# SSD stage with TensorE's small steps further apart, and the second diagonal product in the carried product's PSUM bank

## The chip, the cores and the metric

The kernel runs on one core of one Trainium2 chip, as one launch. The metric is the device time of that core in microseconds (us), as the median of several runs.

## The reference

Two layers of a decoder trunk on 512 tokens of width 1024, in float32. Layer 0 mixes tokens with a Mamba-2 SSD block, layer 1 with an HGRN2 block; each is followed by a layer norm, a squared-ReLU MLP, a second layer norm and a gated embedding. The change touches the SSD block alone:

```
def ssd_mixer(u, ...):                       # u: 512 x 1024; 4 chunks of 128 tokens
    z, xbc, dt = split(u @ w_in)             # z 2048, xbc 2048 + 512 + 512, dt 32 heads
    xs, bm, cm = split(silu(conv4(xbc)))     # causal depthwise convolution of width 4
    dt = softplus(dt + dt_bias); da = dt * -exp(a_log); xdt = xs * dt
    a_cs = cumsum(da) in each chunk
    cb = cm . bm                             # per group (4 groups of 8 heads), 128 x 128
    y_diag = (cb * exp(segsum(da))) @ xdt
    states = bm . (exp(a_cs[-1] - a_cs) * xdt)
    prev = scan over chunks: h * exp(a_cs[-1]) + states
    y_off = cm . prev * exp(a_cs)
    y = (y_diag + y_off + d_skip * xs) * silu(z)
    return rms_norm(y per group of 512) @ w_out
```

## The kernel before

A float32 weight or activation is split into a rounded high part and the rest (`split`, L113 on ScalarE and L115 on VectorE), and each product is made of three matmuls (`mm3`, L119 to L121). Weights come as units of 128x1024 by one load on SyncE's queue, three buffers deep (`raw`), and are copied to six buffers of high and low parts, far ahead of their use.

The SSD block works on channels as rows: 16 tiles of 128 channels (two heads) by 512 tokens. Each tile j has x (`xs`) and the gate (`sz`), made by `xz(j)`: eight steps of `mm3` for x, then convolution (L633 on ScalarE, three L636 on VectorE) and silu (L637), then eight steps for the gate and silu (L697). Each group of four tiles has B and C (`bc_group`, 16 steps) and `bc_prep`: B is transposed (L673) and copied (L675, ScalarE), B·C is multiplied (L679) into bank `py0` and masked (L681, VectorE). `partial(g, h)` is 16 steps of the output product of a finished group, each chunk added to `acc` by L812 on VectorE.

The SSD core of a tile has four small steps on TensorE:

- `enter(j)`: loads the cumulated decays (L709, 512 KB on SyncE's queue), transposes x into bank `pt` (L712); VectorE scales it to `xw` (L718) and `xdt` (L719, two buffers).
- `states(j)`: six matmuls into bank `pm` (L727); VectorE scans them over the chunks (L734, L736, L737); then the decay mask is made (eight L743 on VectorE, L746 on ScalarE, L747 on VectorE) and L752.
- `carried(j)`: multiplies C with the scanned states into bank `py1` (L759); VectorE takes it with L766.
- `diagonal(js)`: for one or two tiles the masked product (L778, 16 matmuls each), the first into `py0`, the second into `pm`; with `rms` the normalizing matmuls of a group follow (L828, bank `pt`, then L832 on ScalarE). VectorE and ScalarE finish y (L791 to L796, L817, L820).

TensorE's order is written by hand in `period(p, work, at)`: the large work is a list of generators that yield after each `mm3` (three matmuls, one unit), and `at` says after which unit which small step is issued. Periods 1 to 8 each take two tiles. In the kernel before, `head(j, n, step)` puts enter, states and carried at units n, n + 4 and n + 8 (with steps of 3 for tile 14). All other engines' instructions are put in order by a scheduler, which works from this order; on each engine they run strictly in that order.

Of the kernel before, what the change touches and what calls it, by code (L numbers as in the profile page):

```python
# [44 lines left out]
def trunk(ctx: ExitStack, tc, a):  # L45
# [13 lines left out]
    psy = pool("psy", 1, space=PSUM)  # L59
    psm = pool("psm", 1, space=PSUM)  # L60
# [7 lines left out]
    def mk(p, shape, tag, dt=F32, **kw):  # L68
        return p.tile(list(shape), dt, tag=tag, name=nm(tag), **kw)
# [19 lines left out]
    def tmp(tag, shape, dt=F32):  # L89
        return mk(phase[0], shape, tag, dt, bufs=phase[2].get(tag, 1))  # L90

    def bank(p, tag):
        return mk(p, [P, T], tag)

    def bc(ap, axis, n):
        v = ap.unsqueeze(axis)
        shape = list(v.shape)
        shape[axis] = n
        return v.to_broadcast(shape)
# [76 lines left out]
    cols, at = {}, 0  # L176
# [479 lines left out]
    def bc_group(g):  # L656
        new = []
        for which in range(2):
            ps = yield from projected(10 * g + which)
            t = tmp(("bm", "cm")[which], [P, T])  # L660
            conv_silu(ps, 16 + 4 * which + g, t)
            new.append(t)
            if g:
                yield
        bcm[:] = new
# [22 lines left out]
    def xz(j):  # L688
        d = tiles[j] = dict()
        ps = yield from projected(10 * (j // 4) + 2 + 2 * (j % 4))  # L690
        d["xs"] = tmp("xs", [P, T])
        conv_silu(ps, j, d["xs"])
        if j:
            yield
        ps = yield from projected(10 * (j // 4) + 3 + 2 * (j % 4))
        d["sz"] = tmp("sz", [P, T])
        nc.scalar.activation(d["sz"], ps, AF.Silu)  # L697
        if j:
            yield
        if j == 4:  # L700
            nc.sync.dma_start(acc, a["x"])
            for c in range(NCH):
                nc.vector.tensor_scalar(acc[:, c, :], acc[:, c, :], ALPHA, None, ALU.mult)

    def enter(j):

        d = tiles[j]
        d["csb"] = mk(w4, [P, 2, T], "a")
        nc.sync.dma_start(d["csb"], bass.AP(tensor=csd.tensor, offset=csd.offset + 2 * j * T, ap=[[0, P], [T, 2], [1, T]]))  # L709
        pt = bank(pst, "pt")  # L710
        for c in range(NCH):
            nc.tensor.transpose(pt[:, c * P : (c + 1) * P], d["xs"][:, c * P : (c + 1) * P], ident)  # L712
        dt_tok, w_tok, _ = toks
        d["xdt"] = tmp("xdt", [P, 8, 64])
        hs = slice(2 * j, 2 * j + 2)
        ptv = pt.rearrange("p (c h q) -> p c h q", c=NCH, h=2)
        d["xw"] = tmp("xw", [P, 3, 2, 64])
        nc.vector.tensor_mul(d["xw"], ptv[:, 0:3], bc(w_tok[:, 0:3, hs], 3, 64))  # L718
        nc.vector.tensor_mul(d["xdt"].rearrange("p (c h) q -> p c h q", c=NCH), ptv, bc(dt_tok[:, :, hs], 3, 64))  # L719

    def states(j):
        d = tiles[j]
        csb, cs_tok = d["csb"], toks[2]
        btok, cbm, cm = prep
        pst_ = bank(psm, "pm")
        for c in range(3):
            nc.tensor.matmul(  # L727
                pst_[:, c * P : (c + 1) * P], btok[:, c, :], d["xw"][:, c].rearrange("p h q -> p (h q)"), start=True, stop=True
            )
        cd = mk(sm, [P, 2, NCH], "cd")  # L730
        nc.scalar.activation(cd, csb.rearrange("p h (c l) -> p h c l", c=NCH)[:, :, :, P - 1], AF.Exp)
        pv = d["pv"] = tmp("pv", [P, 3, 2, 64])
        stv = pst_[:, : 3 * P].rearrange("p (c h q) -> p c h q", c=3, h=2)
        nc.vector.tensor_copy(pv[:, 0], stv[:, 0])  # L734
        for c in range(1, 3):
            nc.vector.tensor_mul(pv[:, c], pv[:, c - 1], bc(cd[:, :, c], 2, 64))  # L736
            nc.vector.tensor_add(pv[:, c], stv[:, c], pv[:, c])  # L737

        m = d["m"] = mk(w4, [P, 2, T], "b")
        for r in range(2):  # L740
            for c in range(NCH):
                sl = slice(c * P, (c + 1) * P)
                nc.vector.tensor_scalar(  # L743
                    m[:, r, sl], csb[:, r, sl], cs_tok[:, c, 2 * j + r : 2 * j + r + 1], 0.0, ALU.subtract, ALU.min
                )
        nc.scalar.activation(m, m, AF.Exp)  # L746
        nc.vector.tensor_mul(m, m, bc(cbm, 1, 2))  # L747

        d["ecs"] = tmp("ecs", [P, 3 * P])
        for r in range(2):  # L750
            rs = slice(64 * r, 64 * r + 64)
            nc.scalar.activation(d["ecs"][rs], csb[rs, r, P:], AF.Exp)  # L752

    def carried(j):
        d = tiles[j]
        cm = prep[2]
        yo = bank(psy, "py1")
        for c in range(1, NCH):
            nc.tensor.matmul(  # L759
                yo[:, c * P : (c + 1) * P],  # L760
                d["pv"][:, c - 1].rearrange("p h q -> p (h q)"),
                cm[:, c * P : (c + 1) * P],
                start=True,
                stop=True,
            )
        nc.vector.tensor_mul(d["ecs"], yo[:, P:], d["ecs"])  # L766
# [3 lines left out]
    def diagonal(js, rms=None):  # L770

        yds = []
        for n, j in enumerate(js):
            yd = bank(psm, "pm") if n else bank(psy, "py0")
            for c in range(NCH):
                sl = slice(c * P, (c + 1) * P)
                for r in range(2):
                    nc.tensor.matmul(  # L778
                        yd[64 * r : 64 * r + 64, sl], tiles[j]["xdt"][:, 2 * c + r, :], tiles[j]["m"][:, r, sl], start=True, stop=True
                    )  # L780
            yds.append(yd)
        if rms is not None:
            groups[rms]["ri"] = rms_group(groups[rms]["ss"])
        for j, yd in zip(js, yds):
            d = tiles.pop(j)
            if j % 4 == 0:
                groups[j // 4] = dict(ys=Split(4), ss=None)
            g = groups[j // 4]
            ys = g["ys"]
            y = tmp("y", [P, T])  # L790
            nc.vector.scalar_tensor_tensor(y, d["xs"], dskip[:, j : j + 1], yd, ALU.mult, ALU.add)  # L791
            nc.vector.tensor_add(y[:, P:], y[:, P:], d["ecs"])
            nc.vector.tensor_mul(y, y, d["sz"])
            w = snw[:, j : j + 1]
            nc.scalar.activation(ys.h(j % 4), y, AF.Copy, scale=w)
            nc.vector.scalar_tensor_tensor(ys.l(j % 4), y, w, f32(ys.h(j % 4)), ALU.mult, ALU.subtract)  # L796
            g["ss"] = sq_sum(y, g["ss"])
# [38 lines left out]
    def period(p, work, at):  # L836

        n = 0
        for item in work:
            for _ in item:  # L840
                n += 1
                for f in at.pop(n, ()):
                    f()
        assert not at, (p, n, at.keys())

    def head(j, n, step=4):
        return {n: [lambda: enter(j)], n + step: [lambda: states(j)], n + 2 * step: [lambda: carried(j)]}

    both = lambda js, rms=None: [lambda: diagonal(js, rms)]
    with tc.manual_schedule(engines={mybir.EngineType.PE}):  # L850
        period(0, [bc_group(0), xz(0), xz(1)], {})
        toks.extend(dt_tail())
        period(1, [xz(2), xz(3)], {8: [bc_prep], **head(0, 12), **head(1, 22)})
        period(2, [bc_group(1), xz(4), xz(5)], {1: both((0, 1)), **head(2, 3), **head(3, 14), 26: [bc_prep], 27: both((2, 3)), **head(4, 37)})
        for p in range(3, 8):
            i, b = 2 * p - 1, p // 2
            if p == 7:
                work = [partial(1, 1), xz(14), xz(15)]
                at = {**head(i, 1), 18: both((i - 1, i), 2), **head(14, 32, 3), 43: both((14,))}
            elif p % 2:  # L860
                work = [xz(i + 1), xz(i + 2)]
                work.insert(1, partial(b - 1, 0))
                at = {**head(i, 1), 15: both((i - 1, i), b - 1), **head(i + 1, 20)}
            else:
                work = [bc_group(b), xz(i + 1), xz(i + 2)]
                if p == 4:
                    work.insert(1, partial(0, 1))
                n = 16 * len(work) - 48
                at = {**head(i, 1), 14: both((i - 1, i)), 26: [bc_prep], **head(i + 1, 35 + n)}
            period(p, work, at)  # L870
        period(8, [partial(2, 0), partial(2, 1)], {**head(15, 1), 14: both((15,))})
    h_s, *after = norm(0)
    out_project(a["wso"][12:16], groups[3]["ys"], False, *after, scale=rms_group(groups[3]["ss"]))
    begin("mlp0")
# [427 lines left out]
```

## Time and profile before

| | us |
|---|---|
| median of 3 runs | 1446.43 (1445.96 to 1446.88) |
| time of the profiled execution | 1448.71 |
| its span, first to last instruction | 1446.8 |
| TensorE busy | 1421.9 |
| VectorE busy | 1055.4 |
| ScalarE busy | 781.8 |
| mean granted TensorE clock | 0.995 of full speed |

A page has the busy time by engine, the span in slices, the DMA queues, the chain that ended last, and groups of instructions with mean time and the idle time before them. In these, PE is TensorE, DVE is VectorE, ACT is ScalarE and SP is SyncE; L712 is line 712 of the kernel. Other answers of the trace are: who waited for whom in a stretch (us in total, times, longest us), busy time by stretch (for TensorE, its weight loads, VectorE, ScalarE and GpSimd, then the granted clock, the share and rate of DMA), groups by line (busy us, mean ns, then idle us before them), and the timeline (start in us, length in us, engine, line, operation, tiles written and read, count).

### The profile page before, as it was taken

The numbers are of one execution on the slowest core, as the hardware profiler recorded it, in microseconds if no ns is written. First come the engines' busy times: TensorE is split into PE (matmuls) and PEld (weight loads), VectorE is DVE, ScalarE is ACT, GpSimd is POOL, SyncE is SP. The second block draws the span as 40 slices with busy tenths as digits, with TensorE's granted clock in tenths as the row PEclk, the third lists the DMA queues.
The fourth block names the chain that finished last, engine by engine and source line by source line (L and its number), as shares of the span: only waits on it lengthen the run. The fifth ranks groups of instructions, "written<-read, shape, count | busy, mean of one in ns | idle before, by whom it ended". The sixth has DMA issues, their size and how long they took to land.

```text
span 1446.8 us, 20044 instructions
## 1 busy us (share of the span) xinstructions
PE 1421.9 (98%) x7869; PEld 1178.3 (81%) x7869; DVE 1055.4 (73%) x1736; ACT 781.8 (54%) x1155; POOL 1.9 (0%) x12
## 2 busy tenths in 40 slices
PE   9999999999999999999999999999999999999998
PEld 7777878787898888888888888787898888888887
DVE  7797768776885867766995756776686776667773
ACT  6777656754345444544554646664555454544551
POOL 0000000000000000000000000000000000000000
PEclk9999999999999999999999999999999999999999
DMA  8422333222443443444622331222162444434231
GB/s 301 147 88 88 117 117 104 101 73 88 174 131 103 146 145 132 145 143 163 218 74 97 104 109 63 85 72 77 59 232 99 144 137 145 146 131 167 95 118 44
DMA packets 49390, 178.00 MB, mean 123 GB/s; under 512 B 5520, under 2 KB 6288, under 8 KB 49168
## 3 DMA queue, kind: packets, MB, share of 16 engines
q1 hardware_dynamic: 49296, 176.73, 36.0%
q8 instruction: 62, 1.02, 0.3%
q14 instruction: 32, 0.26, 0.1%
HBM read 174.54 MB, written 2.16 MB: 122 GB/s over the span
## 4 chain that ended last, share of the span: by engine, by line
PE 88%; DVE 6%; ACT 4%; issue 1%; DMA 1%; SPq 0%; ACTq 0%; DVEq 0%
PE pj L119 22%; PE pj L120 22%; PE pj L121 22%; PE py L119 5%; PE py L121 5%; PE py L120 5%; DVE wlo L115 1%; DVE cv L636 1%; PE py L759 1%; PE py L778 1%; ACT whi L113 1%; PE pm L727 1%; PE pt L233 1%; ACT L637 1%; PE py L1033 1%
## 5 line engine op out<-in xcount | busy, mean ns | idle before, releaser
L113 ACT CAST whi<-raw 128x1024 fp32r<-128x1024 f32 x222 | 233.2, 1051 | 327.7 <-PE pj L120 227.4
L119 PE MATMUL pj<-b,whi 128*128 128x512 f32 (+1 forms) x1006 | 386.4, 385 | 0.7 <-ACT b L237 0.7
L120 PE MATMUL pj<-b,whi 128*128 128x512 f32 (+1 forms) x1006 | 379.9, 378 | 0.4 <-DVE b L238 0.4
L121 PE MATMUL pj<-b,wlo 128*128 128x512 f32 (+1 forms) x1006 | 379.7, 378 | 0.0
L115 DVE TENSOR_TENSOR wlo<-raw,whi 128x1024 fp32r<-128x1024 f32 x222 | 270.3, 1222 | 131.9 <-ACT whi L113 130.7
L121 PEld LDWEIGHTS pj<-b,wlo 128*128 128x128 f32 x1006 | 189.9, 189 | 35.6
L119 PEld LDWEIGHTS pj<-b,whi 128*128 128x128 f32 x1006 | 189.9, 189 | 35.1 <-ACT b L237 0.9
L120 PEld LDWEIGHTS pj<-b,whi 128*128 128x128 f32 x1006 | 190.6, 189 | 33.1 <-DVE b L238 0.6
L119 PE MATMUL pj<-whi,b 128*128 128x512 f32 x536 | 214.2, 400 | 0.0
L121 PE MATMUL pj<-whi,b 128*128 128x512 f32 x544 | 213.1, 393 | 0.0
L120 PE MATMUL pj<-wlo,b 128*128 128x512 f32 x536 | 210.1, 392 | 0.0
L121 PEld LDWEIGHTS pj<-whi,b 128*128 128x128 f32 x544 | 102.3, 188 | 21.5
L119 PEld LDWEIGHTS pj<-whi,b 128*128 128x128 f32 x536 | 101.0, 188 | 20.8 <-ACT b L1160 0.6
L120 PEld LDWEIGHTS pj<-wlo,b 128*128 128x128 f32 x536 | 101.1, 189 | 19.4
L113 ACT CAST whi<-r 128x1024 fp32r<-128x1024 f32 x72 | 75.7, 1053 | 67.7 <-PE pj L121 38.6
L115 DVE TENSOR_TENSOR wlo<-r,whi 128x1024 fp32r<-128x1024 f32 x72 | 87.7, 1221 | 20.4 <-ACT whi L113 19.7
L121 PE MATMUL py<-whi,b 128*128 128x512 f32 (+1 forms) x250 | 97.0, 388 | 0.0
L120 PE MATMUL py<-wlo,b 128*128 128x512 f32 x224 | 87.1, 389 | 0.0
L119 PE MATMUL py<-whi,b 128*128 128x512 f32 x224 | 87.1, 390 | 0.0
L121 PEld LDWEIGHTS py<-whi,b 128*128 128x128 f32 x250 | 46.9, 188 | 9.7
L119 PEld LDWEIGHTS py<-whi,b 128*128 128x128 f32 x224 | 42.0, 188 | 9.1 <-DVE sg L494 0.3
L636 DVE SCALAR_TENSOR_TENSOR cv<-pj,cst,cv 128x509 f32<-128x509 f32 (+2 forms) x66 | 48.7, 745 | 0.7
(296 smaller groups left out, 1874.6 us busy)
## 6 DMA issues: line engine op xcount, KB each, us to landing
raw<-in_w SPq DMA_DIRECT2D x112, 512.0 KB, 3.7
r<-in_w SPq DMA_DIRECT2D x64, 512.0 KB, 4.4
raw<-in_wssd SPq DMA_DIRECT2D x36, 512.0 KB, 4.0
a<-csd SPq DMA_DIRECT2D x16, 512.0 KB, 4.1
raw<-in_wso SPq DMA_DIRECT2D x16, 512.0 KB, 3.7
raw<-in_wg SPq DMA_DIRECT2D x16, 512.0 KB, 3.7
raw<-in_whq SPq DMA_DIRECT2D x16, 512.0 KB, 3.8
raw<-in_whvg SPq DMA_DIRECT2D x14, 512.0 KB, 3.8
```

What stands on the lines that cost most here:

```text
L113: nc.scalar.copy(hi[:, :n], f)
L115: nc.vector.tensor_sub(lo[:, :n], f, f32(hi[:, :n]))
L119: nc.tensor.matmul(out, sh, mh, start=start, stop=False, **kw)
L120: nc.tensor.matmul(out, sh, ml, start=False, stop=False, **kw)
L121: nc.tensor.matmul(out, sl, mh, start=False, stop=stop, **kw)
L233: nc.tensor.transpose(pt[:, j * P : (j + 1) * P], src[:, k * P : (k + 1) * P], ident)
L636: nc.vector.scalar_tensor_tensor(cv[:, d:], ps[:, : T - d], convw[:, i, k : k + 1], cv[:, d:], ALU.mult, ALU.add)
L637: nc.scalar.activation(out, cv, AF.Silu)
L727: nc.tensor.matmul(pst_[:, c * P : (c + 1) * P], btok[:, c, :], d["xw"][:, c].rearrange("p h q -> p (h q)"), start=True, stop=True)
L759: nc.tensor.matmul(yo[:, c * P : (c + 1) * P], d["pv"][:, c - 1].rearrange("p h q -> p (h q)"), cm[:, c * P : (c + 1) * P], start=True, st ...
L778: nc.tensor.matmul(yd[64 * r : 64 * r + 64, sl], tiles[j]["xdt"][:, 2 * c + r, :], tiles[j]["m"][:, r, sl], start=True, stop=True)
L1033: nc.tensor.matmul(pcs[r][bs, n * c : n * c + n], kk[r][:, ts], qs, start=True, stop=True)
```

## The change

`head` and `both` go; a helper `at` takes places (unit, step, arguments). With it each small step of each tile gets a unit of its own: enter to states 6 or 7 units, states to carried 6 to 9, where it was 4 and 4 (3 and 3 for tile 14). The diagonals of a pair move from units 14 to 18 of a period to 25 or 26 (in period 2 from 1 and 27 to 8 and 32); `bc_prep` moves from unit 26 to 34, 41 and 33; in period 7 tile 14's diagonal moves to period 8. Where `partial` stood between the two tiles of periods 3 and 5, it now stands behind them. In periods 2, 3 and 5 a tile is entered before the diagonal of the two tiles ahead of it. The second diagonal product of a pair is put in bank `py1`, which the carried products use, and no longer in `pm`, which the states use.

```diff
@@ -771,7 +771,7 @@
 
         yds = []
         for n, j in enumerate(js):
-            yd = bank(psm, "pm") if n else bank(psy, "py0")
+            yd = bank(psy, "py%d" % n)
             for c in range(NCH):
                 sl = slice(c * P, (c + 1) * P)
                 for r in range(2):
@@ -843,32 +843,41 @@
                     f()
         assert not at, (p, n, at.keys())
 
-    def head(j, n, step=4):
-        return {n: [lambda: enter(j)], n + step: [lambda: states(j)], n + 2 * step: [lambda: carried(j)]}
-
-    both = lambda js, rms=None: [lambda: diagonal(js, rms)]
+    def at(*places):
+
+        plan = {}
+        for n, f, *args in places:
+            plan.setdefault(n, []).append(lambda f=f, args=args: f(*args))
+        return plan
+
     with tc.manual_schedule(engines={mybir.EngineType.PE}):
         period(0, [bc_group(0), xz(0), xz(1)], {})
         toks.extend(dt_tail())
-        period(1, [xz(2), xz(3)], {8: [bc_prep], **head(0, 12), **head(1, 22)})
-        period(2, [bc_group(1), xz(4), xz(5)], {1: both((0, 1)), **head(2, 3), **head(3, 14), 26: [bc_prep], 27: both((2, 3)), **head(4, 37)})
+        plan = at((8, bc_prep), (10, enter, 0), (16, states, 0), (20, enter, 1), (25, carried, 0), (26, states, 1))
+        period(1, [xz(2), xz(3)], plan)
+        plan = at((1, carried, 1), (2, enter, 2), (8, diagonal, (0, 1)), (10, states, 2), (14, enter, 3), (18, carried, 2), (20, states, 3))
+        plan |= at((28, carried, 3), (32, diagonal, (2, 3)), (34, bc_prep), (37, enter, 4), (44, states, 4))
+        period(2, [bc_group(1), xz(4), xz(5)], plan)
         for p in range(3, 8):
             i, b = 2 * p - 1, p // 2
-            if p == 7:
-                work = [partial(1, 1), xz(14), xz(15)]
-                at = {**head(i, 1), 18: both((i - 1, i), 2), **head(14, 32, 3), 43: both((14,))}
-            elif p % 2:
+            if p % 2:
                 work = [xz(i + 1), xz(i + 2)]
-                work.insert(1, partial(b - 1, 0))
-                at = {**head(i, 1), 15: both((i - 1, i), b - 1), **head(i + 1, 20)}
+                work.insert(0 if p == 7 else 2, partial(*((1, 1) if p == 7 else (b - 1, 0))))
+                plan = at((2, carried, i - 1), (5, enter, i), (12, states, i), (19, carried, i), (25, diagonal, (i - 1, i), b - 1))
+                if p < 7:
+                    plan |= at((17, enter, i + 1), (27, states, i + 1), (36, carried, i + 1))
+                else:
+                    plan |= at((31, enter, 14), (37, states, 14), (44, carried, 14))
             else:
                 work = [bc_group(b), xz(i + 1), xz(i + 2)]
                 if p == 4:
                     work.insert(1, partial(0, 1))
                 n = 16 * len(work) - 48
-                at = {**head(i, 1), 14: both((i - 1, i)), 26: [bc_prep], **head(i + 1, 35 + n)}
-            period(p, work, at)
-        period(8, [partial(2, 0), partial(2, 1)], {**head(15, 1), 14: both((15,))})
+                plan = at((5, enter, i), (12, states, i), (20, carried, i), (26, diagonal, (i - 1, i)))
+                plan |= at((33 + n // 2, bc_prep), (37 + n, enter, i + 1), (44 + n, states, i + 1))
+            period(p, work, plan)
+        plan = at((1, diagonal, (14,)), (4, enter, 15), (10, states, 15), (16, carried, 15), (20, diagonal, (15,)))
+        period(8, [partial(2, 0), partial(2, 1)], plan)
     h_s, *after = norm(0)
     out_project(a["wso"][12:16], groups[3]["ys"], False, *after, scale=rms_group(groups[3]["ss"]))
     begin("mlp0")
```

## The prediction

> **What bounds the kernel now.** I read the first part of the page, then who waited for whom on TensorE, then busy time by stretch, then the timeline at the longest waits.
>
> ```profile
> span 1446.8 us, 20044 instructions
> PE 1421.9 (98%) x7869; PEld 1178.3 (81%) x7869; DVE 1055.4 (73%) x1736; ACT 781.8 (54%) x1155; POOL 1.9 (0%) x12
> ```
>
> TensorE has work for all but 24.9 us of the span, so no other engine sets the end; a change of order can only win back TensorE's idle time and time in which its matmuls run slower than they could. The change touches only the SSD stage, whose hand-ordered part with small steps lies between about 45 and 345 us. TensorE's waits there:
>
> ```profile
> PE py L759 <- DVE pv L737: 5.4, 7, 1.7
> PE py L679 <- ACT cm L637: 5.1, 2, 2.6
> PE pt L712 <- ACT xs L637: 3.9, 3, 3.3
> PE pm L727 <- DVE xw L718: 0.8, 2, 0.4
> PE py L778 <- DVE cbm L681: 0.2, 1, 0.2
> ```
>
> So 15.4 us of waiting in 15 stops, all at small matmuls that were placed too soon after the work that feeds them: the carried part (L759) after the scan of states (L737), the B·C product (L679) after C's silu, the entry (L712) after x's silu. Busy time by stretch shows a second price:
>
> ```profile
> 70.00:105.00 35.00, 33.57 (x214) 27.80 (x214) 32.55 (x70) 27.06 (x37) 0.00 (x0) 1.00 0.27 91
> 105.00:125.00 20.00, 18.06 (x84) 14.78 (x83) 15.95 (x34) 17.07 (x20) 0.00 (x0) 0.91 0.35 112
> 178.00:192.00 14.00, 11.49 (x50) 9.50 (x49) 11.51 (x26) 9.71 (x13) 0.00 (x0) 0.88 0.25 76
> 276.00:287.00 11.00, 8.39 (x36) 6.91 (x35) 8.83 (x22) 10.87 (x13) 0.00 (x0) 0.84 0.53 184
> 322.00:340.00 18.00, 14.66 (x66) 12.03 (x65) 13.86 (x30) 10.82 (x14) 0.00 (x0) 0.91 0.28 89
> ```
>
> The granted clock (the third figure from the end, 1.00 in the first row) falls in the four stretches that hold the long waits: 20 x 0.09 + 14 x 0.12 + 11 x 0.16 + 18 x 0.09 = 6.9 us of clock. The timeline of one of them:
>
> ```profile
> 109.54 0.83 PE L727 MATMUL pm<-xw,btok 128*128 128x128 f32 x6
> ...
> 112.30 0.39 PE L119 MATMUL pj<-b,whi 128*128 128x512 f32 x1
> 112.53 0.39 PE L120 MATMUL pj<-b,whi 128*128 128x512 f32 x1
> ...
> 112.98 0.38 PE L759 MATMUL py<-cm,pv 128*128 128x128 f32 x2
> 113.60 0.49 PE L759 MATMUL py<-cm,pv 128*128 128x128 f32 x2 [0.24 <-DVE pv L737]
> 115.80 0.49 PE L759 MATMUL py<-cm,pv 128*128 128x128 f32 x2 [1.71 <-DVE pv L737]
> 116.04 0.47 PE L119 MATMUL pj<-b,whi 128*128 128x512 f32 x1
> ...
> 117.32 0.63 PE L120 MATMUL pj<-b,whi 128*128 128x512 f32 x1
> 117.74 0.63 PE L121 MATMUL pj<-b,wlo 128*128 128x512 f32 x1
> ```
>
> Starts are 0.23 us apart before the wait (three make a unit of 0.68 us, the step by which the order is counted) and 0.42 apart after it: the matmuls run at about half speed for some 3 us. Counted in matmuls the loss is about 6.5 us at the four places, and I take that, since a little of the 6.9 lies inside the waits. A stop also breaks the pipeline: six L727 in a row take 0.83 us, 0.11 each and 0.28 for the last, so the restart costs 0.28 - 0.11 = 0.17, 2.6 us for 15 stops. What the stage can give back is 15.4 + 6.5 + 2.6 = 24.5 us.
>
> [...]
>
> **The change part by part.** No matmul is added or removed. The number of places where small matmuls break the stream stays about the same, so the switch back to large ones (0.47 instead of 0.39 us at 116.04) costs the same. The units below are the list's own counts.
>
> (1) The B·C product goes from unit 26 to unit 34, 41 and 33 of periods 2, 4 and 6. Its two long waits have one cause:
>
> ```profile
> 182.25 0.48 ACT L675 COPY btok<-pt 128x384 f32<-128x384 f32 x1 [0.93 <-PE pt L673]
> 182.75 1.28 ACT L637 ACT_TABLE_LOAD   x1
> 184.04 0.63 ACT L637 ACTIVATE cm<-cv 128x512 f32<-128x512 f32 x1
> ```
>
> ScalarE stands at L675, which waits for TensorE's transposes of the same step; only behind it come a table load and C's silu, which TensorE then waits for. In the built order of the changed program C's silu stands well before L675 in all three periods, so both waits, 5.1 us, and 3.4 of clock go.
>
> (2) Tile 14's entry waited 3.3 us because on ScalarE its silu stood behind the gate's:
>
> ```profile
> 329.06 1.28 ACT L697 ACT_TABLE_LOAD   x1
> 330.36 0.60 ACT L697 ACTIVATE sz<-pj 128x512 f32<-128x512 f32 x1
> 330.85 0.62 ACT L637 ACTIVATE xs<-cv 128x512 f32<-128x512 f32 x1
> ```
>
> The changed order has x's silu first, but behind L832, which waits for the normalizing matmuls of unit 25. The lengths of a pair of diagonals and of the normalizing matmuls (48 of them in 1.9 us, 16 at a time):
>
> ```profile
> 70.84 1.09 PE L778 MATMUL py<-b,xdt 128*64 128x128 f32 x16
> ...
> 72.74 0.50 PE L119 MATMUL pj<-b,whi 128*128 128x512 f32 x1
> ```
>
> ```profile
> L828 PE MATMUL pt<-ones_s,ss 128*64 128x64 f32 x48 | 1.9, 222 | 0.0
> ```
>
> Counted from the diagonal's start, its 32 matmuls take 1.9 and the 16 of L828 end at 2.4; on ScalarE then come L832 0.26, a load 1.28, L752 0.53, a load 1.28 and the silu 0.62: 6.4. TensorE is at unit 31 after 2.5 + 6 x 0.68 = 6.6. It just fits. Price if not: each late 0.1 is a 0.1 wait, and clock only from about 1.7.
>
> (3) States to carried: 4 units before (3 for tile 14), 6 to 9 now, that is 2.7 us against 4.1 to 6.1. What has to fit is VectorE's queue, which is where the price lies:
>
> ```profile
> L115 DVE TENSOR_TENSOR wlo<-raw,whi 128x1024 fp32r<-128x1024 f32 x42 | 51.2, 1221 | 20.1 <-ACT whi L113 20.1
> L636 DVE SCALAR_TENSOR_TENSOR cv<-pj,cst,cv 128x509 f32<-128x509 f32 (+2 forms) x60 | 44.6, 745 | 0.6
> L743 DVE TENSOR_SCALAR b<-a,toks 128x128 f32<-128x128 f32 x119 | 27.4, 284 | 0.0
> L747 DVE TENSOR_TENSOR b<-b,cbm 128x1024 f32<-128x1024 f32 x16 | 19.5, 1221 | 3.2 <-ACT b L746 3.2
> L719 DVE TENSOR_TENSOR xdt<-pt,toks 128x512 f32<-128x512 f32 x15 | 10.2, 681 | 0.0
> L737 DVE TENSOR_TENSOR pv<-pm,pv 128x128 f32<-128x128 f32 x30 | 8.7, 290 | 0.5
> L718 DVE TENSOR_TENSOR xw<-pt,toks 128x384 f32<-128x384 f32 x15 | 8.3, 555 | 15.5 <-PE pt L712 15.3
> L791 DVE SCALAR_TENSOR_TENSOR y<-xs,cst,py 128x512 f32<-128x512 f32 x8 | 6.0, 744 | 6.7 <-PE py L778 6.7
> ```
>
> Packed, each starts 0.09 before the last ends: L115 and L747 take 1.13, L636 and L791 0.66, L719 0.60, L743 and a scan step 0.2; L766, L792 and L793 are of L718's and L719's size, L796, L812 and L820 of L791's and L719's. The method, tried on the kernel before at tile 4 (entry at 0): L718, L719, L820 and eight L743 end at 3.8, L734 4.15, L747 5.3, L636, L736, L636, L737 7.0, L636, L736, L115, L737 9.3. TensorE reaches the carried part at 6.8, its second pair 7.0, its third 7.35: waits of 0.2 and 1.95, where the rows at 113.60 and 115.80 have 0.24 and 1.71. It is good to 0.3.
>
> On the changed order, tile 4 again (states 7 units after the entry, carried 6 on): L718 ends at 1.35, L820 2.45 (it waits for ScalarE's square), L719 and seven L743 4.4, three L636 with L743 and L115 between 7.75, L734 7.95, L747, L736, L115, L737 10.6, two more scan steps with L743 between 11.5. TensorE arrives at 10.2 and 10.6: waits of 0.3 and 0.5 instead of 1.95 and the clock. Tile 14 (7 units) has two L115 inside its scan that wait for ScalarE's copies; the same sum gives 0.85. Tiles 2 and 3 come out within 0.3 of no wait, tile 6 is in (5), the others have 1 us or more to spare.
>
> (4) The second diagonal part goes to the carried part's bank. It no longer holds the states' bank. In exchange it needs L766 to have read the bank, and the next carried part needs L791: the nearest such pairs are 4 units and 10 units apart, 2.7 and 6.8 us against reads of 0.56 and 0.74. Cost 0, at most 0.2 at tile 3.
>
> (5) In periods 2, 3 and 5 the next tile is now entered before the diagonal. Its L719 needs a third buffer of two, so VectorE stands from about unit 20 to the diagonal at 25 (period 2: 4 to 8), 3 to 3.5 us, with everything behind it: the convolution's L636, L791, the scan of tile 6. The normalizing matmuls wait for L719 as well (one transposes' bank): it starts when the first 16 of 32 matmuls are done, 1.1, and ends at 1.8; TensorE is there at 1.9. Then, from the diagonal: L636, L791, L636, L792, L636, L833, L793, L791 to 6.2, the scan between L792, L793 and L743 to 8.7. TensorE comes to tile 6's carried part at 2.4 + 11 x 0.68 + 0.9 = 10.8. Spare 2.1. The entries of tiles 6 and 10 at unit 17 come 0.6 after their silus. Cost 0, up to 3.5 a place if the sums are off.
>
> (6) The entry's load of 512 KB moves with it on SyncE's queue, past a weight tile here and there.
>
> ```profile
> a<-csd SPq DMA_DIRECT2D x16, 512.0 KB, 4.1
> ```
>
> It is issued when the tile two before is done; at 4.1 us to landing it lands level with or before ScalarE's need. Cost 0 to 1.2 on ScalarE, where it holds L731 and what follows; tile 3's diagonal (unit 32) then waits 0.2.
>
> Sum: of 24.5, what stays is 0.8 + 0.85 + 0.3 + 0.2 with restarts of 0.17 each, about 2.8; for the close fits I add 0.7. Gain 21. The profiled execution took 1448.7, its span 1446.8; the median is 1446.4, 2.3 below the profiled one. From the median: 1446.4 - 21 = 1425.4.
>
> **The rivals.** (a) The waits move instead of going. VectorE has little room: 32.55 of 35 us in the stretch from 70 on, and (5) takes 3 us from it there. If the sums are 2 us short at five of the seven close places (tiles 2, 3, 4, 14; entries 6, 10, 14), waits of 2 us with 0.17 and half of the clock price, 0.8, cost 5 x 3 = 15 in place of 3.5: gain 9.5, 1437. [...] For it: seven fits under 0.7. Against: the method erred by 0.3, to the side of too much wait. (b) Slower: the hold of (5) is not made good. In periods 2, 3 and 5, and the two after 3 and 5 that inherit the queue, TensorE stands w at the carried part and pays 1.7 of clock: 5 x (w + 1.7) exceeds 24.5 from w = 3.2. With w = 5, a whole hold and half of another, 33.5 - 24.5 makes it 9 us slower, 1455. Against: the 2.1 spare, and 300 - 228.7 us of free VectorE over the stage:
>
> ```profile
> 45.00:345.00 300.00, 284.53 (x1556) 234.41 (x1555) 228.67 (x447) 194.95 (x243) 0.00 (x0) 0.98 0.31 101
> ```
>
> (c) Nothing to measure: what is won is lost to the copies of weights, which TensorE now reaches sooner. They are made a good eight units ahead, and VectorE would be at 228.7/279, 82%. Then 1446.
>
> **How the numbers follow.** Forecast 0.64 (1421 to 1431), (a) 0.24 (1431 to 1442), (c) 0.04, (b) 0.08. The predicted time is the forecast's, 1425. The low end is a gain of all 24.5 and a little of switching, 1421; the high end, 1438, takes most of (a) and leaves out its last 0.06, (c) and (b), 0.18. Changes of up to 0.2%, 2.9 us, can't be told from none: faster 0.88, same 0.04, slower 0.08.
>
> **What would show it.** Right: TensorE's waits in this stage under 4 us, none at L679, granted clock 0.99 to 1.00 in every stretch, the stage some 21 us shorter, nothing changed after it. (3) wrong: L759 on L737 over 2 us. (5) wrong: a wait at L828 on L719, or L759 waits in periods 3 and 5. (2) wrong: L712 on L637. Wrong altogether: waits of 15 us or more, or a clock under 0.95 in new places.

## The result, and the profile after

The changed kernel takes 1427.44 us (median, 1426.19 to 1428.45) beside 1446.66 for the kernel before on the same chip: ratio 0.9863, 95% interval 0.9846 to 0.988, a gain of 19.2 us. Run again, as e8, beside e9 to e11 it took 1427.45, ratio 0.9853 (0.9838 to 0.9867), a gain of 20.8. Forecast were 21 us and 1425.4; the range held.

First the page, then who waited for whom on TensorE in the SSD stage (us in total, times, longest), both of the kernel after:

```profile
span 1424.4 us, 20036 instructions
PE 1411.9 (99%) x7869; PEld 1172.3 (82%) x7869; DVE 1053.8 (74%) x1736; ACT 778.6 (55%) x1153; POOL 1.9 (0%) x12
```

```profile
PE py L759 <- DVE pv L737: 2.7, 4, 1.0
PE pt L828 <- DVE xdt L719: 0.5, 2, 0.3
```

The same matmuls are there. Of 15 stops with 15.4 us of waits, six with 3.2 us are in this answer; one more of 0.13 stands in tile 3's diagonal. The waits of L679, L712 and L727 are gone. Busy time over the whole stage shows the second part of the gain, the granted clock, third from the end:

```profile
45.00:325.00 280.00, 276.69 (x1550) 229.87 (x1550) 226.40 (x442) 192.96 (x242) 0.00 (x0) 1.00 0.33 108
```

It is 1.00 now; in the kernel before it was 0.98 over the stage, with 0.91, 0.88, 0.84 and 0.91 in the four stretches with long waits. Where the stage begins, and behind it, both timelines show the same matmuls, first before, then after:

```profile
46.80 0.38 PE L673 MATMUL pt<-cst,bm 128*128 128x128 f32 x2
...
372.36 0.45 PE L828 MATMUL pt<-ones_s,ss 128*64 128x64 f32 x8
```

```profile
45.71 0.49 PE L673 MATMUL pt<-cst,bm 128*128 128x128 f32 x3
...
350.34 0.45 PE L828 MATMUL pt<-ones_s,ss 128*64 128x64 f32 x8
```

The spans differ by 22.4 us (1446.8 and 1424.4), and 20.9 of them lie in the stage. Another 1.1 lie ahead of it, where the change does nothing: in the other profiles, of either order, L673 begins between 45.5 and 46.8. What is left in the timeline of after (PEld is TensorE's weight load):

```profile
84.71 0.49 PE L759 MATMUL py<-cm,pv 128*128 128x128 f32 x2 [1.01 <-DVE pv L737]
...
113.41 0.38 PE L759 MATMUL py<-cm,pv 128*128 128x128 f32 x2
114.30 0.49 PE L759 MATMUL py<-cm,pv 128*128 128x128 f32 x2 [0.51 <-DVE pv L737]
115.09 0.49 PE L759 MATMUL py<-cm,pv 128*128 128x128 f32 x2 [0.30 <-DVE pv L737]
...
309.40 0.42 PEld L712 LDWEIGHTS pt<-cst,xs 128*128 128x128 f32 x4 [0.35 <-ACT xs L637]
309.40 0.65 PE L712 MATMUL pt<-cst,xs 128*128 128x128 f32 x4
...
320.98 0.49 PE L759 MATMUL py<-cm,pv 128*128 128x128 f32 x2 [0.88 <-DVE pv L737]
```

Tile 2's carried part waits 1.0, tile 4's 0.5 and 0.3, tile 14's 0.9. Tile 14's entry at 309.40 has no wait of its matmuls, but its weight load was held by x's silu; point (2) below comes back to it.

### The profile page after: what moved, and what is told of

The parts are those of the page before. It is cut to its first block, busy times and chain, and to the rows that moved or that the text cites. A ratio compares the mean times of both kernels' runs of the same rounds, so it can differ in the third digit from the quotient of the medians.

```text
span 1424.4 us, 20036 instructions
## 1 busy us (share of the span) xinstructions
PE 1411.9 (99%) x7869; PEld 1172.3 (82%) x7869; DVE 1053.8 (74%) x1736; ACT 778.6 (55%) x1153; POOL 1.9 (0%) x12
## 4 chain that ended last, share of the span: by engine, by line
PE 93%; DVE 5%; ACT 2%; issue 0%; DVEq 0%; ACTq 0%
PE pj L119 24%; PE pj L120 23%; PE pj L121 23%; PE py L119 5%; PE py L121 5%; PE py L120 5%; DVE wlo L115 1%; PE pt L233 1%; PE py L759 1%; PE pm L727 1%; PE py L1042 1%; PE py L1148 1%; ACT whi L113 0%; DVE cv L636 0%; PE py L778 0%; PE pt L712 0%
## 5 line engine op out<-in xcount | busy, mean ns | idle before, releaser
L113 ACT CAST whi<-raw 128x1024 fp32r<-128x1024 f32 x222 | 233.0, 1051 | 316.8 <-PE pj L120 227.5
L115 DVE TENSOR_TENSOR wlo<-raw,whi 128x1024 fp32r<-128x1024 f32 x222 | 269.9, 1220 | 142.5 <-ACT whi L113 141.0
L113 ACT CAST whi<-r 128x1024 fp32r<-128x1024 f32 x72 | 75.7, 1053 | 67.7 <-PE pj L121 38.5
L115 DVE TENSOR_TENSOR wlo<-r,whi 128x1024 fp32r<-128x1024 f32 x72 | 87.6, 1219 | 20.0 <-ACT whi L113 19.2
L636 DVE SCALAR_TENSOR_TENSOR cv<-pj,cst,cv 128x509 f32<-128x509 f32 (+2 forms) x66 | 48.5, 742 | 5.6 <-ACT cv L633 5.3
```

Source lines behind the costliest of these rows:

```text
L113: nc.scalar.copy(hi[:, :n], f)
L115: nc.vector.tensor_sub(lo[:, :n], f, f32(hi[:, :n]))
L636: nc.vector.scalar_tensor_tensor(cv[:, d:], ps[:, : T - d], convw[:, i, k : k + 1], cv[:, d:], ALU.mult, ALU.add)
```

## The experiments

The diffs show only the parts of lines that change; the remarks in them are added.

### The bank alone, put in and taken out

e1 is the kernel before with the second diagonal product in the other bank; e2 is the kernel after with that line undone.

```diff
-            yd = bank(psm, "pm") if n else bank(psy, "py0")     # e2 turns this round
+            yd = bank(psy, "py%d" % n)
```

> The kernel before with one line changed: the second diagonal product goes to the carried product's bank. Theory (the prediction's step 4: the bank costs and wins nothing by itself; in the old order the states follow a diagonal by 4 units or more): no measurable change, 1446 +- 1 us, the same 15 stops of TensorE in the SSD stage with 15 us of waits. Rival (the states' bank was a hidden brake in the old order): 2 us or more faster. Rival (the carried product now waits for VectorE's read of the second diagonal): slower by 1 us or more, seen as waits at L759 that L791 ends.

Measured: 1448.8, ratio 1.0005 (0.9996 to 1.0013) to the kernel before. No change, as expected. The long waits are those of before; the small ones differ somewhat (16.6 us in 13 stops in all).

> The changed kernel with that one line undone: the second diagonal product goes back to the states' bank. In periods 2, 3 and 5 of the new order states follow the pair's diagonal by 2 units, 1.36 us. Theory (step 4, the hold of the bank is real in the new order): by step 5's sum the second L791 ends 6.2 us after the diagonal's start and TensorE is at the states after 3.8 us (2.4 + 2 units), so 2.4 us of wait at L727 at each of two places, some 2.5 in period 2, and half speed after each as after the 1.71 us wait of before: 7.5 + 0.5 + 5 = 13 us slower than the changed kernel, near 1440; without the clock loss 1435. Rival (L791 comes much earlier, the bank never mattered): 1427, no wait at L727.

Measured: 1435.98, ratio to before 0.9923 (0.9911 to 0.9936): 8.5 us slower than after (on another chip; by the two ratios to before 8.7). TensorE's longest waits in e2, and busy time around two of them:

```profile
PE pm L727 <- DVE y L791: 7.8, 3, 3.6
PE py L759 <- DVE pv L737: 0.9, 1, 0.9
```

```profile
138.00:150.00 12.00, 9.67 (x65) 7.72 (x62) 12.00 (x36) 10.16 (x14) 0.00 (x0) 1.00 0.16 48
230.00:245.00 15.00, 12.66 (x84) 10.23 (x81) 14.29 (x37) 13.12 (x17) 0.00 (x0) 0.89 0.22 71
```

The three waits came where expected and sum to 7.8 for 7.5. Two things are smaller: the waits of tiles 2 and 4, 1.0 and 0.8 in after, are gone (that VectorE catches up while TensorE stands at L727 is the author's reading); and one of the three waits costs no clock (1.00 in the first row, beside 0.89 in the second and 0.86 from 76 to 88 us). With 0.5 us at tile 4's entry and 0.5 at L828, e2 waits 9.7 us in 7 stops, 6.4 more than after in as many; two losses of clock at 1.6 make it 9.6. So the line is worth nothing in the old order and 8.5 us in the new one, where the states follow a diagonal by two units.

### The B·C product alone

```diff
-26: [bc_prep], 27: both((2, 3)), **head(4, 37)
+27: both((2, 3)), 34: [bc_prep], **head(4, 37)
...
-26: [bc_prep], **head(i + 1, 35 + n)
+33 + n // 2: [bc_prep], **head(i + 1, 35 + n)
```

> The kernel before with only the B.C product moved, from unit 26 to 34, 41 and 33 of periods 2, 4 and 6. Theory (step 1): both waits of L679 for C's silu go, 5.1 us, their clock loss of 3.4 and two restarts: 8.8 us faster, 1437.7, granted clock 1.00 where it was 0.88 and 0.84. [...] Rival (ScalarE's copy still stands ahead of C's silu, or another wait comes): under 3 us faster.

Measured: 1437.34, ratio 0.9931 (0.9918 to 0.9945), 9.8 us faster. In e3's waits no L679 is left, and the clock is whole where the two waits had been:

```profile
PE py L759 <- DVE pv L737: 4.1, 6, 1.2
PE pt L712 <- ACT xs L637: 3.9, 3, 3.3
```

```profile
178.00:192.00 14.00, 14.00 (x68) 11.71 (x68) 11.69 (x24) 10.62 (x13) 0.00 (x0) 1.00 0.49 164
276.00:287.00 11.00, 10.29 (x58) 8.68 (x57) 10.32 (x21) 6.00 (x8) 0.00 (x0) 1.00 0.65 204
```

This is nearly half of the gain. 9.8 are nearer to the theory's 8.8 than to the 5.1 + 2 x 0.17 = 5.4 of the waits and restarts without clock: the waits of 2.5 and 2.6 us had cost clock, 0.88 and 0.84 in these two stretches before and 1.00 now. The rest of the 9.8 is in other waits: L759 has 4.1 us in place of 5.4, and tile 4's entry a new one of 0.7.

### What held tile 14's entry

e4 puts tile 14's steps one unit earlier in the kernel before, which turns round the two silus on ScalarE. e5 leaves them and moves the pair's diagonal.

```diff
-18: both((i - 1, i), 2), **head(14, 32, 3)
+18: both((i - 1, i), 2), **head(14, 31, 3)     # e4
+25: both((i - 1, i), 2), **head(14, 32, 3)     # e5
```

> The kernel before with only tile 14's three small steps one unit earlier (31, 34, 37 in place of 32, 35, 38). In the built order this puts x's silu of tile 14 ahead of the gate's silu on ScalarE, with a table load less between. Theory (step 2: the 3.3 us wait was the order on ScalarE, not the distance, so an earlier place can wait less): the wait at L712 goes, 3.3 + 1.6 of clock + 0.2 = 5 us; steps of 3 units stay, so up to 1 us comes back at L759: 4 to 5 us faster, 1442. Rival (the distance sets it): an earlier entry waits 0.7 us longer, 1447.

Measured: 1448.35, ratio 1.001 (1.0001 to 1.0019): not faster. TensorE and ScalarE in e4, then VectorE in the kernel before:

```profile
331.26 1.12 PE L712 MATMUL pt<-cst,xs 128*128 128x128 f32 x4 [4.10 <-ACT xs L637]
```

```profile
329.28 1.28 ACT L637 ACT_TABLE_LOAD   x1 [2.52 <-DVE cv L636]
330.57 0.63 ACT L637 ACTIVATE xs<-cv 128x512 f32<-128x512 f32 x1
```

```profile
328.80 0.76 DVE L636 SCALAR_TENSOR_TENSOR cv<-pj,cst,cv 128x511 f32<-128x511 f32 x1
```

ScalarE now stands idle for 2.5 us ahead of x's silu, waiting for the convolution on VectorE. In the kernel before the last L636 ends at 329.56; with a table load of 1.28 and 0.62 of silu x cannot be there before 331.46, and it was there at 331.47. In e4 the load waited for L636 as the silu does, so with the gate's silu out of the way x is there no sooner, and the earlier entry just waits longer. The gate's silu ahead of it had cost nothing.

> The kernel before with one number changed: in period 7 the pair's diagonal stands at unit 25 in place of 18; tile 14's steps stay at 32, 35 and 38. e4 put x's silu first on ScalarE and the wait grew from 3.34 to 4.10 us, so ScalarE's order, the reason of step 2, is not what holds it: VectorE's convolution L636 ended after the pair's ten long instructions. Theory (VectorE's queue: a diagonal seven units before the convolution puts all of its tail ahead of it; a diagonal beside it lets the three L636 go between): the 3.3 us wait at L712 goes with its clock, 1446 - 4.5 = 1441 to 1442. Rival (the order of the two silus on ScalarE after all): the wait stays over 3 us, 1446. Rival (the tail comes back at the carried step, whose scan now stands behind it): L712 goes, up to 2 us come at L759, 1443 to 1444.

Measured: 1444.36, ratio 0.998 (0.9971 to 0.9989), 2.9 us faster. e5's waits up to 350 us:

```profile
PE py L759 <- DVE pv L737: 6.4, 7, 1.7
...
PE pt L712 <- ACT xs L637: 1.1, 3, 0.6
```

The 3.3 us wait is gone, with nothing changed at tile 14. With its diagonal at unit 18, L791 to L820 stood ahead of the convolution on VectorE; at 25 the three L636 are put between them. Part of the tail comes back, as the last rival said: 1.1 us at tile 14's carried part and 0.6 at the next entry. In the changed kernel, with longer steps, tile 14's carried part still waits 0.9 and the next entry no more. There VectorE and ScalarE come to x at the same moment:

```profile
306.60 0.74 DVE L636 SCALAR_TENSOR_TENSOR cv<-pj,cst,cv 128x511 f32<-128x511 f32 x1
306.79 0.53 ACT L752 ACTIVATE ecs<-a 64x384 f32<-64x384 f32 x1
```

The last L636 ends at 307.34 and L752, behind which x's silu stands, at 307.32; the silu's table load starts at 307.42.

### The distances alone

e6 is the changed kernel with states 4 units after the entry and the carried part 4 after the states. Most tiles of the changed kernel have 6 or 7 units from entry to states; tile 2 has 8 and tiles 6 and 10 have 10, and e6 leaves these three. One of its lines:

```diff
-plan = at((2, carried, i - 1), (5, enter, i), (12, states, i), (19, carried, i), (25, ...
+plan = at((5, enter, i), (9, states, i), (13, carried, i), (25, ...
```

> The changed kernel with the distances of before: states 4 units after the entry and the carried part 4 after the states, at the changed places of entries, diagonals and of the B.C product. Left at their changed places are the states and carried parts of tiles 6 and 10, whose scaling waits for a diagonal, and the states of tile 2. Theory (step 3: the distance is worth what its waits of before were worth, 5.4 us in 7 stops with restarts and some clock, less the 2.7 that stay): 5 to 8 us slower than the changed kernel, 1432 to 1435, all at L759 on L737. Rival (with diagonals and B.C moved VectorE's queue is free enough, the distance is worth nothing): 1427 to 1428. Rival (VectorE's tails now hit the scans): 10 us slower or more, 1437.

Measured: 1440.07, ratio to before 0.995 (0.9938 to 0.9963): 12.6 us slower than after, as the last rival said (10 or more); the theory's 5 to 8 was too little. e6's waits:

```profile
PE py L759 <- DVE pv L737: 9.2, 21, 1.2
PE pt L712 <- ACT btok L675: 0.5, 1, 0.5
PE pt L828 <- DVE xdt L719: 0.5, 2, 0.3
PE py L759 <- DVE pv L734: 0.4, 1, 0.4
```

That is 10.6 us in 25 stops, 7.3 us and 18 stops more than after, and no clock lost. The waits alone don't make 12.6; the stops have a price of their own, and it is higher than the 0.17 of the prediction. Rows 113.41 and 114.30 of after show it: a pair of L759 takes 0.38 without a stop and 0.49 with one. So besides the prediction's 0.17 for the last matmul ahead of a stop (0.28 for 0.11), the first pair after it takes 0.11 longer: an estimated 0.28 a stop, and 7.3 + 18 x 0.28 = 12.3.

### Waits of chosen length

> The changed kernel with four carried parts put earlier, to make waits of known length: tile 6 at 29 (was 36), tile 10 at 30 (was 36), tiles 8 and 12 one unit after their states. By the spare of the changed trace the waits should be some 2.0, 1.4, 1.1 and 1.5 us, 6.0 in all. What it tells: whether a wait's length alone sets the loss of clock. In before, e1 and e4 one wait of 1.70 us at the same place lost clock in two of three profiles, in e2 2.03 lost none and 2.14 did. Theory (a wait under some 2.5 us loses clock or not by where it falls, so the loss differs between waits of like length): 6 + 4 x 0.17 and 0 to 2 losses of 1.7: 7 to 10 us slower than the changed kernel, 1434 to 1437. Rival (a length of about 1.7 decides): one loss, at tile 6 alone. Rival (a wait costs no more than its length): 1433.

Measured: 1434.51, ratio 0.9912 (0.9897 to 0.9927), 7.1 us slower than after. e7's waits:

```profile
PE py L759 <- DVE pv L737: 6.6, 12, 1.0
PE pt L828 <- DVE xdt L719: 0.5, 2, 0.3
PE py L759 <- DVE pv L734: 0.4, 2, 0.2
```

It missed its purpose. The scans end as long after their states as in the changed kernel (4.6 us at tile 6, 3.0 at tile 8, in both), but a carried part's three pairs of matmuls wait for three steps of the scan in turn, so each long wait falls into two or three pieces, none over 1.0. They fit the price of a stop: 7.5 us in 16 stops, 4.2 and 9 more than after (its 0.13 counted), 4.2 + 9 x 0.28 = 6.7 for 7.1 measured, without any loss of clock.

### Towards a better order

e9 puts three carried parts later, e10 adds a buffer, e11 does both with other places, e12 is e11 without the buffer. e8, the changed kernel again, ran beside the first three.

```diff
-(18, carried, 2), (20, states, 3)        (44, carried, 14)
+(20, carried, 2), (20, states, 3)        (46, carried, 14)                    # e9, e11, e12
-(2, carried, i - 1)
+(4 if p == 3 else 2, carried, i - 1)     # e9
+(5, carried, i - 1)                      # e11, e12
-(17, enter, i + 1)
+(19, enter, i + 1)                       # e11, e12
-xs=4, sz=4, xdt=2
+xs=4, sz=4, xdt=3                        # e10, e11
```

> The changed kernel itself, beside the three that follow, so that differences of 1 to 4 us are read on one chip. 1427 us, ratio 0.986.

> The changed kernel with three carried parts later: tile 2 at 20 (was 18), tile 4 at 4 (was 2), tile 14 at 46 (was 44). Theory: a wait costs its length and 0.27 of restart (e6 and e7: 0.16 for the last matmul to drain and 0.11 for the first), so the waits of 1.0, 0.5 + 0.3 and 0.9 with four restarts go: 3.7 us faster than the changed kernel, 1423.7. Rival (what comes later on VectorE moves with them and another step waits, as the tail did in e5): under 1.5 us faster.

Measured: 1429.65, ratio 0.987 (0.9854 to 0.9886), 2.2 us slower than after in place of 3.7 faster. Neither the theory nor the rival, which still had it faster, was right. e9's longest waits, ScalarE ahead of the first of them, and busy time around it:

```profile
PE pt L712 <- ACT xs L637: 2.2, 1, 2.2
PE pm L727 <- DVE xw L718: 1.3, 1, 1.3
```

```profile
125.07 1.05 ACT L113 CAST whi<-raw 128x1024 fp32r<-128x1024 f32 x1 [4.43 <-PE pj L120]
...
127.43 0.63 ACT L637 ACTIVATE xs<-cv 128x512 f32<-128x512 f32 x1
```

```profile
125.00:135.00 10.00, 7.82 (x34) 6.26 (x33) 3.10 (x6) 4.95 (x6) 0.00 (x0) 0.83 0.32 105
```

All of L759's waits went, and two others came: TensorE got to tile 3's states sooner than L718, and tile 6's silu now stands on ScalarE behind a weight copy that waits for TensorE. The 2.2 us wait also cost clock (0.83), which the changed kernel doesn't lose in its stage. A step moved by hand also moves what the scheduler puts on the other engines.

> The changed kernel with three buffers of xdt in place of two, so that L719 need not wait for the diagonal in periods 2, 3 and 5. In the changed trace VectorE stands still before the diagonal (70 to 75 us), but by the row there L115 waits for its weight copy, and L719 starts as L115 ends. Theory (L115 is the brake, not L719): the two waits at L828 go, 0.5 + 2 x 0.27, tile 2's wait shrinks by L719's 0.68 and no more: 1.7 us faster, 1425.7, and VectorE still stands some 3 us there. Rival (step 5: L719 holds VectorE): VectorE's idle time goes from that place, tile 2's wait goes whole, 2.3 us faster, 1425.1, and the carried parts of tiles 6 and 10 have 3 us more spare than 2.2 us.

Measured: 1426.74, ratio 0.985 (0.9835 to 0.9864), 0.7 us under e8, less than its own runs differ (1425.5 to 1428.7): the time can't tell theory from rival, the rows can. VectorE in period 2, first the kernel after, then e10:

```profile
74.02 1.22 DVE L115 TENSOR_TENSOR wlo<-raw,whi 128x1024 fp32r<-128x1024 f32 x1 [2.92 <-ACT whi L113]
75.17 0.68 DVE L719 TENSOR_TENSOR xdt<-pt,toks 128x512 f32<-128x512 f32 x1
```

```profile
72.55 0.68 DVE L719 TENSOR_TENSOR xdt<-pt,toks 128x512 f32<-128x512 f32 x1
...
77.06 1.23 DVE L115 TENSOR_TENSOR wlo<-raw,whi 128x1024 fp32r<-128x1024 f32 x1 [2.35 <-ACT whi L113]
```

With L719 free to go first, VectorE still stands, 2.35 us, at the low part's copy L115, which waits for ScalarE's L113. L719 was not the brake. The spare at tile 6 shows it too: from the end of the last L737 to its carried part it is 2.3 us (144.41 to 146.72) where the changed kernel has 2.2 (142.55 to 144.75), and the rival wanted 3 more. The waits at L828 are gone, and tile 2's is 0.42 for 1.01. The profile of e10 also has a wait of 2.1 us at tile 0's entry that after's has not, behind a weight copy whose load came late (L113 at 42.79 waits 2.05 us for it). Two buffers have such a wait there as well, 0.7 in e8 and in e1, so it is not put down to the third.

> Both together: three buffers of xdt, the carried parts of tiles 2 and 14 later as in the run before, the carried parts of tiles 4, 8 and 12 together with the next entry at unit 5, the entries of tiles 6 and 10 together with a carried part at unit 19, so that six breaks in the stream of large matmuls go at some 0.1 us each. 3.7 + 1.0 + 0.6 = 5 us faster than the changed kernel, 1422. Rival (entries at 19 press on the states of tiles 6 and 10 or L759 waits again): 1424.

> The kernel of the run before (e11) with two buffers of xdt again, so its moves of steps alone. It tells which half of e11 won 4.5 us over the changed kernel, where e9's moves lost 2 and e10's third buffer won 0.7. Theory (places decide, and e9 lost by two next steps with little spare, L727 at tile 3 and the entry of tile 6, which e11 puts at 19): 1423.5 to 1424.5, with the two waits at L828 back, 0.5 + 2 x 0.27. Rival (the third buffer is what makes room on VectorE for the moves): 1427 or more, with waits of over 1 us at L727 of tile 3 and at tile 6's entry.

Measured: e11 1422.9, ratio 0.9823 (0.9809 to 0.9838), 4.5 us under e8; e12 1423.98, ratio 0.9835 (0.982 to 0.9849), on another chip. e11's waits, then e12's:

```profile
PE pt L712 <- ACT xs L637: 0.8, 1, 0.8
PE pm L727 <- DVE xw L718: 0.7, 1, 0.7
```

```profile
PE pm L727 <- DVE xw L718: 1.3, 1, 1.3
PE pt L712 <- ACT xs L637: 0.8, 1, 0.8
PE pt L828 <- DVE xdt L719: 0.5, 2, 0.3
```

The places do most of it: e12 has 0.6 of what e11 wins over e8 by the ratios, 0.8 by the medians. e9's new waits are there again, but tile 6's is 0.8 in place of 2.2, since its entry is two units later, and costs no clock. e11 is faster than both kernels of this case: two stops are left in the stage.

## Why the prediction was right, point by point

- **Bound and size.** TensorE's idle and slow time were all there was to win. Measured 19.2 and 20.8 for 21. The sum with the right price of a stop: before 15.4 + 6.5 + 15 x 0.28 = 26.1, after 3.3 + 7 x 0.28 = 5.3, gain 20.8; the stages of the two profiled runs differ by 20.9. The predicted restart of 0.17 was mis-sized on both sides of the sum, and only 8 x 0.11 = 0.9 of that is left. But the sum takes four losses of clock from the profiled run of before and subtracts them from the median, and most runs lose three (see Clock): from the median it is 1.6 less, 19.2. That 21 came as near as it did is in part luck.
- **(1) B·C product.** Right and shown by e3: 9.8 for 8.8. That L675 is what holds C's silu is read from the trace, not tried by itself.
- **(2) Tile 14's entry.** The outcome was nearly right: no wait that the lists show, but no spare either. The matmul ahead started at 309.09, and at the other entries L712 starts 0.23 behind it, which would be 309.32; the silu ended at 309.35 and L712 started at 309.40, 0.08 late, for a spare of 0.2 forecast. The reason failed. The step took the gate's silu, next to the wait in ScalarE's timeline, for its cause; e4 took it away and the wait grew to 4.1. VectorE's queue was the cause, and moving the diagonal removes the wait (e5). The step added up ScalarE's queue alone; that VectorE's convolution ended with it, at 307.34 beside 307.32, is luck.
- **(3) Distances.** Tile 4 was predicted at 0.3 + 0.5 and has 0.5 + 0.3, tile 14 at 0.85 and has 0.88, tile 3's diagonal at 0.2 and has 0.13. Tile 2 was put within 0.3 of no wait and has 1.01; that comes from (5). In this order the distances are worth 12.6 us (e6), though in the kernel before L759 waited only 5.4: the new places of entries and diagonals need them.
- **(4) The bank.** Cost 0, as e1 shows for the old order. The step didn't price what the bank holds off: 8.5 us (e2).
- **(5) VectorE's hold.** Cost 0 was nearly right, 0.5 at L828 and 0.7 more than allowed at tile 2, but the hold was put down to the wrong instruction. The sum had L719 end 1.8 us after the diagonal's start, 74.9 in period 2 (the diagonal starts at 73.06); it ended at 75.85, because L115 stands ahead of it and waits for its copy. e10 shows that without L719's wait VectorE still stands. The rest of the sum held: tile 6's scan ended 9.0 us after the diagonal's start for 8.7, and TensorE came at 11.2 for 10.8.
- **(6) The entry's load.** No wait in the trace is put down to it, and none at L759 needs it to be explained.
- **Clock.** That the low clock hangs on the waits is shown (e3). That each wait above 1.7 us costs its 1.6 is not so; see below. Tile 4's loss in the profiled run of before was not bound to come: e1 has the same wait without it. One loss, 3.41 us at half speed, takes 3.41 x 0.5 / 1447 = 0.0012 off the mean granted clock of a run, so by this estimate 0.995 stands for four, as in the profiled runs of before and e4, and 0.996 for three. On the chip of e1 to e4, 13 of 21 runs of before have 0.996 and take 1446.8 on average, eight have 0.995 and take 1449.4. The 2.3 us that the prediction saw between the profiled run and the median are of this size.
- **Rivals.** (a) did happen, in e9: waits moved on to the next close fit. In the changed kernel the places were far enough apart. (b) did not come: VectorE did stand, 2.9 us in period 2 and 3.7 in period 3, but tile 6's spare of 2.2 was left. (c) did not come either.

## What to carry to other kernels

When one engine is full and its order is set by hand, price a stop as its length plus a fixed part (0.28 us here) and count stops as well as microseconds: 25 small ones cost more here (e6, 12.6 us) than three long ones (e2, 8.5). Before naming the instruction next to a wait as its cause, ask when the input of the late one was ready, and follow it to the engine that made it. A step moved on one engine rebuilds the queues of the others, so the next close fit has to be looked up in the built order of each version.

## What the hardware showed that was not expected

The loss of clock doesn't go by the length of a wait alone. Tile 4's wait of 1.7 us was followed by half speed in the profiles of before and e4 (granted clock 0.91 from 105 to 125 us in both) and of e5, and not in e1, where the instructions around it are the same and the large ones go on 0.32 and then 0.23 us apart, as they do in after behind the stops at 84.71 and 115.09:

```profile
117.52 0.49 PE L759 MATMUL py<-cm,pv 128*128 128x128 f32 x2 [1.70 <-DVE pv L737]
117.76 0.48 PE L119 MATMUL pj<-b,whi 128*128 128x512 f32 x1
118.08 0.39 PE L120 MATMUL pj<-b,whi 128*128 128x512 f32 x1
```

Busy time by stretch, narrowed to where the granted clock is 0.50, shows how long half speed lasts. In the kernel before:

```profile
116.70:120.11 3.41, 3.41 (x10) 2.66 (x9) 1.77 (x3) 3.15 (x4) 0.00 (x0) 0.50 0.62 185
184.97:188.38 3.41, 3.41 (x13) 3.02 (x13) 1.83 (x7) 2.06 (x2) 0.00 (x0) 0.50 0.79 250
280.54:283.95 3.41, 3.41 (x13) 3.02 (x14) 3.11 (x10) 3.37 (x4) 0.00 (x0) 0.50 0.47 163
331.74:335.15 3.41, 3.41 (x11) 2.83 (x10) 2.38 (x3) 2.09 (x2) 0.00 (x0) 0.50 0.54 161
```

Each lasts 3.41 us. Starts of large matmuls are 0.227 us apart at full and 0.427 at half speed, so one such stretch costs 3.41 x (1 - 0.227 / 0.427) = 1.6 us. The ends are 68.27, 95.57 and 51.20 us apart, 20 x 3.414, 28 x 3.413 and 15 x 3.413: they lie on a grid of that length. In e4 the four ends lie on such a grid too, shifted by half a microsecond. Counting the idle time in each step of the grid, 1.94 us (before, tile 4) and 1.88 (e5, tile 4) brought half speed in the next step, and 1.25 (e1, tile 4), 1.65 (e2, the 2.04 us wait, cut by the grid) and 1.70 (e10, the 2.1 us wait at tile 0, cut by the grid) did not. Counted so in all fourteen profiles, each of the 18 losses follows a step with at least 1.88 us idle, and no step with 1.70 or less is followed by one. In before the steps ahead of its four stretches have 1.94, 2.51, 2.61 and 3.20 us idle and no other up to 1440 us has over 1.22. So in these profiles the 1.6 us of clock went after a step with 1.88 us or more idle and never after one with 1.70 or less, and waits of up to 1.3 us never cost it.
